# Tables for the order of each engine's instructions in the two attention layers of a trunk kernel

## The chip, the cores and the metric

One core of a Trainium2 chip runs the whole program. The metric is the device time of one execution in microseconds (us), the median over several executions. The engines are TensorE (PE: matmuls; PEld: its weight loads, which run beside the matmuls), VectorE (DVE), ScalarE (ACT), GpSimd (POOL) and SyncE (SP, which here only issues DMAs). Each engine takes its instructions strictly in the order in which they stand in its own stream and waits at the head of the stream until the operands of the next one are ready.

## What is computed

The input is x of 512 tokens by 1024 features. Two layers follow, an even one and an odd one, and each is a mixer and a feed-forward network (FFN) with an RMS norm ahead of both:

```python
for layer in range(DEPTH):                      # DEPTH = 2
    h = rms_norm(x, norm_mix_g[layer])
    x = x + (even_mixer if layer % 2 == 0 else odd_mixer)(h, ...)
    h = rms_norm(x, norm_ffn_g[layer])
    x = x + swiglu(h, ffn_w1[layer], ffn_w3[layer], ffn_w2[layer])
```

The even mixer has an attention of 8 heads in which each query sees only its 128 best keys, chosen by an index score (`relu(qi . ki)` summed over 4 index heads with weights `wi`), and a pooling of the projection `u` over windows of 2, 4, 8 and 16 tokens. The odd mixer has a stick-breaking attention of 16 heads: with `z = q . k`, the weight of a key is `exp(log_sigmoid(z) - sum of softplus(z) over the later keys)`. All products have fp32 inputs.

## The kernel before, in words

**Data.** x lies transposed in eight chunks `xs[0..7]` of 128 features by 512 tokens. Each fp32 operand of a large product is split into a high and a low part, and a product is three matmuls (high by high L205, high by low L206, low by high L207; in the FFNs L526 to L528 with 256 columns). Weights come by DMA on SP into three `raw` buffers, and are split by L177 to L181 and L188 in the mixers and L410/L411 in the FFNs.

**The norm.** `Norm.squared` adds the squares of the chunks on POOL (L280). `stats` multiplies the sum by ones on PE (L286), `ms` on DVE (L288) adds epsilon, and POOL takes the power of -1/2 into `rcol` (L291). `bcast` spreads `rcol` over the partitions with four matmuls (L297), and DVE copies that into `rb` (L307). Products run on the unscaled x, and `rb` is applied to what they give. For the FFN's norm, POOL and DVE also take sums and differences of the chunk pairs (L352 to L355), which the FFN's products read (L358).

**The even mixer** is a list of steps (`EVEN_ORDER`, L52), walked at L979. After the index projections `qi` and `ki` come `st` (stats) and `sb` (bcast), then `kj` (the index keys, scaled by `rb`), and `z(b)`: the scores of the query block b, of which there are four of 128. `sel(b, part)` finds the best 128 keys in 16 rounds of a maximum of eight (L770) and a replacement (L771) on DVE. `q(c, i)`, `nat` and `kn` make the queries, values and keys, `u(g, i)` and `y(g)` the pooling. `s(b, j, c)` is the score product of a block and head (L874 to L876), its maximum (L879, DVE), its exponential (L882, ACT) and its scaling; `pt` transposes it, `av` (L225, the helper `Bank.mm`) multiplies it with the values. `op(n)` adds the pooling's part of the output projection to chunk n, `oa(n)` the attention's part, and `oa(n)` then calls `chunk(n)` of the FFN's norm, from which its sums and squares start.

**The odd mixer** is a second list (`ODD_ORDER`, L74), walked at L1205. For each of eight chunks c of two heads there are `q(c, i)` and `k(c, i)` (24 matmuls each for both halves), `z(c, part)` for three parts A, B and C of the lower triangle, `e` (the softplus on ACT, DVE and POOL, split into `sh` and `sl`, L1139), `s` (the sum over later keys, matmuls that read `sh` and `sl`), `f` and `a` (the exponential, split into `ah` and `al`, L1167) and `o` (the product with the values). `x(h, n)` is the output projection.

**What sets the order.** The lists give the order in which the program is traced. The instructions of each engine are then laid out by the scheduler of the framework, which simulates the engines and takes, of the instructions that are ready, the one traced first. `follow` (L209) pins one instruction behind another on its engine without a semaphore. The FFN uses it once: `bcast` takes `after` (L293, called at L630), so that the four matmuls of `bcast` stand behind the products that `m` names.

Of the kernel before, what the change touches and what calls it, by code (L numbers as in the profile page):

```python
# [104 lines left out]
]  # L105
NEG = -1e30
GONE = -3e38
GONE_TEST = -2.5e38
# [8 lines left out]
def tile_trunk(ctx, tc, x, gains, qk_gain, pool_scale, w_a, w_nat, pool_w, w_o0, w_qk, w_v, w_o1, w13, w2, out):  # L117
    nc = tc.nc
    te, ve, ac, gp = nc.tensor, nc.vector, nc.scalar, nc.gpsimd
# [16 lines left out]
    def take(banks=range(8), n=1):  # L136

        free = [b for b in banks if all(i in given for i in range(b, b + n))]
        b = min(free, key=lambda b: max(given[i] for i in range(b, b + n)))
        ps = psum[:, b, :] if n == 1 else psum[:, b : b + n, :]  # L140
        for i in range(b, b + n):
            del given[i]
        taken[id(ps)] = ps, range(b, b + n)
        return ps

    def give(ps):
        for b in taken.pop(id(ps))[1]:
            given[b] = next(clock)
# [60 lines left out]
    def follow(m, first, why):  # L209

        tc.add_manual_dep(
            m.ins,
            first.ins.name,
            mybir.DependencyInfo(mybir.DependencyClass.NoSync, mybir.DependencyReason.DATA),
            reason=why,
        )
# [24 lines left out]
    class Norm:  # L241
# [48 lines left out]
            self.rcol = stat.tile([P, NB], F32, name=f"rcol{i}", tag="rcol")  # L290
            gp.tensor_tensor(self.rcol, ms, mhalf[:, 0:NB], op=ALU.pow)  # L291

        def bcast(self, banks=range(8), after=None):  # L293
            i = self.idx
            pb = take(banks)
            for b in range(NB):
                m = te.matmul(  # L297
                    pb[:, b * P : (b + 1) * P],
                    self.rcol[:, b : b + 1].to_broadcast([P, P]),
                    ident,  # L300
                    start=True,
                    stop=True,
                )
                if after is not None:
                    follow(m, after, "behind products that wait for less")
            self.rb = stat.tile([P, T], F32, name=f"rb{i}", tag="rb")
            ve.tensor_copy(self.rb, pb)  # L307
            give(pb)
# [53 lines left out]
    class Ffn:  # L362
# [13 lines left out]
        def open(self):  # L376
            self.nraw, self.nsplit = 0, 0
            self.fr = self.pool("fr", 1)
            self.fw = self.pool("fw", 2)
            self.fs = self.pool("fs", 1)  # L380
            self.steps = ffn(self)
# [20 lines left out]
    def ffn(stage):  # L402
        layer, nrm, nxt = stage.layer, stage.nrm, stage.nxt
# [219 lines left out]
        for f in range(1, NP):  # L623
            for w in range(2):
                x = Job(f, w)
                for who, p in ((x, 1), (x, 2), (y, 4), (x, 6), (y, 3), (x, 5), (x, 7)):
                    if who is not None:
                        m = who.prod(p)
                    elif p == 4:
                        nrm.bcast(after=m)  # L630
                        for d in start:
                            d.done()
                y = x
                q, r = divmod(f, 2)
                if q:
                    Down(q - 1, 2 * r + w)
# [13 lines left out]
    def even(nrm, nxt, w_first, after):  # L650
        with ExitStack() as es_wk:
# [23 lines left out]
            for j in range(2):  # L675
# [3 lines left out]
            gp.affine_select(  # L679
                bias[0], bias[0], pattern=[[-1, P]], base=0, channel_multiplier=1, compare_op=ALU.is_ge, fill=NEG  # L680
            )
# [84 lines left out]
            def step_sel(b, part):  # L766
# [5 lines left out]
                if part == NSEL // 32 - 1:  # L772
                    ve.tensor_scalar(bias[b], sc, GONE_TEST, NEG, op0=ALU.is_gt, op1=ALU.mult)

# [469 lines left out]
    ffns[1].run()  # L1244


# [1 line left out]
def _station(w):  # L1248

    k, m = w.shape  # L1250
    return w.reshape(k // 128, 128, m // 128, 128).transpose(2, 1, 0, 3).reshape(m // 128, 128, k)
# [51 lines left out]
```

## Time and profile before

| | |
|---|---|
| median of 3 runs | 1184.28 us (1182.9 to 1185.0) |
| the profiled execution's own time | 1183.68 us |
| span of its trace | 1181.9 us |
| granted TensorE clock, mean | 0.993 of full |
| busy: PE, PEld, DVE, ACT, POOL | 1143.6, 1005.8, 862.1, 606.1, 547.9 us |

The profiled execution lies 0.6 us below the median, and 1.8 us of it lie around the span. The even mixer fills the first 235 us or so, its FFN the time to about 540 us, the odd mixer that to about 860 us, and the second FFN the rest. Matmuls are pipelined, so one of 512 columns is shown with some 390 ns though the next one starts about 230 ns after it; a stretch in which PE is busy throughout can still hold matmuls that start late.

### The profile page before, as it was taken

To read this page: it belongs to the slowest core of one execution; us is meant where nothing else is said; L and a number is where in the kernel's file an instruction comes from. 1 tells how busy PE (TensorE), PEld (TensorE's weight loads), DVE (VectorE), ACT (ScalarE), POOL (GpSimd) and SP (SyncE) were. 2 spreads that over 40 slices of the span, in tenths; PEclk is the share of its full clock that TensorE was granted. 3 is DMA by queue.
4 is the path that set the end of the run, shared out by engine and by line. 5 is a ranking of instruction groups with operands and counts; after the bars stand their busy time and mean duration, and the time that the engine had idled before them with its cause. 6 is when DMAs were issued, how large, how long until landed. Compare 5 with 4: busy or idle time off the path is not lost.

```text
span 1181.9 us, 17814 instructions
## 1 busy us (share of the span) xinstructions
PE 1143.6 (97%) x6854; PEld 1005.8 (85%) x6856; DVE 862.1 (73%) x1180; ACT 606.1 (51%) x929; POOL 547.9 (46%) x506
## 2 busy tenths in 40 slices
PE   7998989999999999999999999999799999999998
PEld 4885747799999999998888888888699999999997
DVE  7699936688778677757467778877678877676764
ACT  5354566454444444436257788866354444444441
POOL 4166646766444444403033345434876444454420
PEclk9999999899999999999999999999999999999999
DMA  5221112123333333323321111114122332333321
GB/s 202 74 87 59 54 36 95 48 90 108 108 107 93 102 105 94 108 73 97 106 94 45 52 36 54 54 54 127 34 90 87 111 109 96 100 108 108 108 90 71
DMA packets 37667, 102.60 MB, mean 87 GB/s; under 512 B 4560, under 2 KB 7120, under 8 KB 37584
## 3 DMA queue, kind: packets, MB, share of 16 engines
q1 hardware_dynamic: 37152, 101.47, 27.5%
q8 instruction: 53, 0.87, 0.3%
q14 instruction: 30, 0.25, 0.1%
q10 hardware_dynamic: 432, 0.02, 0.0%
HBM read 99.37 MB, written 2.10 MB: 86 GB/s over the span
## 4 chain that ended last, share of the span: by engine, by line
PE 73%; DVE 9%; POOL 8%; issue 5%; ACT 3%; DMA 1%; SPq 0%; POOLq 0%; DVEq 0%; ACTq 0%
PE psum L526 10%; PE psum L528 10%; PE psum L527 10%; PE psum L205 10%; PE psum L206 10%; PE psum L207 10%; PE psum L225 6%; DVE score L771 1%; DVE m L770 1%; PE psum L1027 1%; PE psum L1028 1%; PE psum L1029 1%; POOL acc L280 1%; POOL s L494 1%; POOL s L492 1%
## 5 line engine op out<-in xcount | busy, mean ns | idle before, releaser
L599 DVE TENSOR_TENSOR x<-x,psum 128x512 f32<-128x512 f32 x88 | 60.4, 686 | 119.6 <-PE psum L207 119.4
L492 POOL TENSOR_TENSOR s<-raw_w 128x512 f32<-128x512 f32 x40 | 60.2, 1505 | 178.8 <-DMA raw_w<-in_w_dram 154.1
L206 PE MATMUL psum<-gsl,wh_w 128*128 128x512 f32 x352 | 137.7, 391 | 0.0
L207 PE MATMUL psum<-gsh,wl_w 128*128 128x512 f32 x352 | 135.4, 390 | 0.0
L205 PE MATMUL psum<-gsh,wh_w 128*128 128x512 f32 x352 | 135.2, 391 | 0.0
L577 POOL TENSOR_TENSOR c<-c,rb 128x512 f32<-128x512 f32 x40 | 61.2, 1530 | 118.3 <-ACT c L576 118.3
L410 ACT CAST wh_w<-raw_w 128x1024 fp32r<-128x1024 f32 (+1 forms) x48 | 47.0, 980 | 114.5 <-PE psum L206 106.6
L526 PE MATMUL psum<-hh,wh_t 128*128 128x256 f32 x320 | 90.1, 282 | 0.5 <-DVE c L559 0.5
L526 PE MATMUL psum<-hh,wh_a 128*128 128x256 f32 x320 | 90.1, 282 | 0.5 <-ACT wh_a L410 0.5
L528 PE MATMUL psum<-hh,wl_s 128*128 128x256 f32 x320 | 90.3, 283 | 0.0
L526 PE MATMUL psum<-hh,wh_s 128*128 128x256 f32 x320 | 90.3, 283 | 0.0
L527 PE MATMUL psum<-hl,wh_t 128*128 128x256 f32 x320 | 90.3, 282 | 0.0
L527 PE MATMUL psum<-hl,wh_s 128*128 128x256 f32 x320 | 89.9, 281 | 0.0
L527 PE MATMUL psum<-hl,wh_a 128*128 128x256 f32 x320 | 89.8, 281 | 0.0
L528 PE MATMUL psum<-hh,wl_t 128*128 128x256 f32 x320 | 89.7, 280 | 0.0
L528 PE MATMUL psum<-hh,wl_a 128*128 128x256 f32 x320 | 89.6, 281 | 0.0
L410 ACT CAST wh_a<-raw_w 128x1024 fp32r<-128x1024 f32 x40 | 42.0, 1050 | 71.8 <-PE psum L206 57.4
L207 PEld LDWEIGHTS psum<-gsh,wl_w 128*128 128x128 f32 x352 | 66.2, 188 | 12.9
L206 PEld LDWEIGHTS psum<-gsl,wh_w 128*128 128x128 f32 x352 | 66.2, 188 | 12.1
L205 PEld LDWEIGHTS psum<-gsh,wh_w 128*128 128x128 f32 x352 | 65.8, 188 | 11.8
L411 DVE TENSOR_TENSOR wl_a<-raw_w,wh_a 128x1024 fp32r<-128x1024 f32 x40 | 65.8, 1646 | 12.9 <-ACT wh_a L410 12.9
L411 DVE TENSOR_TENSOR wl_w<-raw_w,wh_w 128x1024 fp32r<-128x1024 f32 (+1 forms) x48 | 64.6, 1346 | 3.6 <-ACT wh_w L410 3.5
(357 smaller groups left out, 3780.7 us busy)
## 6 DMA issues: line engine op xcount, KB each, us to landing
raw_w<-in_w_dram SPq DMA_DIRECT2D x88, 512.0 KB, 3.6
raw_w<-in_w_dram SPq DMA_DIRECT2D x80, 256.0 KB, 3.0
raw_v<-in_w_v_dram SPq DMA_DIRECT2D x8, 512.0 KB, 3.7
raw_q<-in_w_qk_dram SPq DMA_DIRECT2D x8, 512.0 KB, 3.6
raw_k<-in_w_qk_dram SPq DMA_DIRECT2D x8, 512.0 KB, 3.7
raw_o<-in_w_o_dram SPq DMA_DIRECT2D x8, 512.0 KB, 3.6
x<-in_x_dram SPq DMA_DIRECT2D x8, 256.0 KB, 4.7
raw_q<-in_w_a_dram SPq DMA_DIRECT2D x4, 512.0 KB, 4.8
```

What stands on the lines that cost most here:

```text
L205: te.matmul(ps, wh, ah, start=(first and i == 0), stop=False)
L206: te.matmul(ps, wh, al, start=False, stop=False)
L207: te.matmul(ps, wl, ah, start=False, stop=(last and i == n - 1))
L225: m = te.matmul(dst, lhsT, rhs, start=self.first is None, stop=stop, skip_group_check=True)
L410: ac.copy(h[:, :n], src)
L411: ve.tensor_sub(l[:, :n], src, f32(h[:, :n]))
L492: gp.tensor_add(z[0], a21, a22)
L526: te.matmul(ps, wh, ah, start=first, stop=False, skip_group_check=True)
L527: te.matmul(ps, wh, al, start=False, stop=False, skip_group_check=True)
L528: m = te.matmul(ps, wl, ah, start=False, stop=(k == KC // 2 - 1), skip_group_check=True)
L577: gp.tensor_mul(d, d, nrm.rb)
L599: ve.tensor_add(xs[n], xs[n], self.ps[i])
```

## The change

The change adds a dictionary `ENGINE_ORDER` with one table for each engine, and at the end of the program, after everything is traced, pins each instruction that a table names behind the one that the table names before it, in the manner of `follow`. The numbers count the instructions of that engine in the order of tracing. `after` and its loop go from `bcast`. No instruction is added or taken away, and no operand changes.

The tables hold 3199 of the 6784 matmuls that are traced on PE, 662 of 1132 instructions on DVE, 560 of 890 on ACT, 355 of 507 on POOL and 110 of 314 on SP. Nearly all of the FFN's instructions are left out: on PE the table skips 1167 to 3107 almost entirely, and all from 5152 on. The order of SP's table is the one that SP had before. The matmuls of `bcast` of both FFN norms (932 to 935 and 4596 to 4599) are in the table.

```diff
+ENGINE_ORDER = {
+    "PE": (
+        "0-21 24-25 22-23 48-49 26-36 50-53 37-39 54-59 72 40-47 60-61 73-75 62-71 76-79 188-199 208-212 86 "
+        "84 90 88 80 87 89 81-83 85 91 213-219 104-112 232 128-130 233 131-133 113-115 152 92-93 116-127 "
...
+        "706-709 705 710-711 702-704 736 748 712 724-725 760 772 761 713-714 737-747 762-771 749-759 726 "
+        "715-723 727-735 773-778 808 779 811 780-781 809 812-813 782-783 823 796-797 784-785 824-825 835 810 "
...
+        "870 930-931 897 874 872-873 877-879 898 902-903 880-883 905-907 904 875-876 972-973 932-935 948 "
...
+        "3820 3735 3750-3751 3821-3825 3788 3826 3796 3740 3827-3831 3797-3798 3741-3742 3799-3802 3743 "
+        "3789-3794 3803-3806 3812-3817 3807-3809 3795 3744-3747 3856-3857 3818 3810 3858-3863 3836-3837 3811 "
...
+        "4551-4553 4557-4559 4563 4561 4564 4533 4582 4562 4566 4583 4567-4568 4594 4534 4544-4547 4538-4540 "
+        "4565 4569-4570 4595 4571 4500-4501 4511 4612-4613 4512-4513 4523-4525 4529-4531 4535-4536 4614-4617 "
+        "4600-4604 4596-4599 4537 4541-4542 4648 4618-4622 4543 4605-4611 4636-4638 4696-4697 4623 4649-4652 "
...
+    "DVE": (
+        "1 0 16-18 15 19 3-4 2 14 5-13 22 25 38-39 20-21 40 26 23 41-42 24 27 30 28-29 31-36 56 37 47 57 48 "
+        "68-75 81-88 95 58 96-98 59 99-102 123-131 43 89 44-45 60-61 105 46 62 52 143-144 49-50 115 53 51 "
...
+    "Pool": (
...
+        "111 110 106 115 120 112-113 147 114 148 129 116-118 138 121 123 122 125 124 126-128 130 132 131 "
+        "133-134 136 135 137 155 139 156 142 144 143 145 157 150-151 153 146 167-170 149 161 152 159-160 162 "
+        "154 158 163-166 173-176 172 179-180 171 181-182 177 185 183-184 186 178 270-272 277 276 278 273 279 "
...
+        "367 363-366 368-370 373 371-372 374 376-378 375 379-380 382-383 381 384-385 387 386 389 388 391 407 "
+        "405-406 408 390 395 393 392 396 394 401 399 397-398 400 402-404 411-412 409 413-414 410 417-420 416 "
...
-        def bcast(self, banks=range(8), after=None):
+        def bcast(self, banks=range(8)):
...
-                m = te.matmul(
+                te.matmul(
...
-                if after is not None:
-                    follow(m, after, "behind products that wait for less")
...
-                        nrm.bcast(after=m)
+                        nrm.bcast()
...
+    traced = [m for m in nc.cur_bb.bb.instructions]
+    for engine, runs in ENGINE_ORDER.items():
+        own = [m for m in traced if m.engine == getattr(mybir.EngineType, engine)]
+        places = []
+        for run in runs.split():
+            first, _, last = run.partition("-")
+            places += range(int(first), int(last or first) + 1)
+        for a, b in zip(places, places[1:]):
+            tc.add_manual_dep(
+                own[b],
+                own[a].name,
+                mybir.DependencyInfo(mybir.DependencyClass.NoSync, mybir.DependencyReason.DATA),
+                reason="order of the engine",
+            )
```

What the numbers of the lines shown stand for:

| engine | numbers: step |
|---|---|
| PE | 0-23 qi(0), 24-47 qi(1), 48-71 ki, 72-75 st, 76-79 sb, 80-83 kj, 84-91 z(1), 188-199 q(0,0), 208-219 q(0,1) |
| PE | 693-704 op(7), 705 and 710-711 last av, 712-723 oa(0), 724-735 oa(1), 736-747 oa(2), 748-759 oa(3), 760-771 oa(4), 772-783 oa(5), 796-807 oa(7), 808-879 and 884-907 the FFN's first two whole products, 880-883 its stats, 908-931 the next products, 932-935 its bcast |
| PE | 3740-3747 s(3,C), 3788-3803 s(3,B), 3804-3819 s(3,A), 3820-3831 k(4,1), 3856-3867 q(5,0) |
| PE | 4544-4547 stats of the second FFN, 4596-4599 its bcast |
| DVE | 27 rb copy, 28-29 the norm's square (L718, L719), 30 kif (L725), 34-37 z(1), 41-42 split of q_0, 56-57 split of q_1, 47-48 q(0,1), 68-75 and 81-88 and 95-102 and 123-130 sel(1, 0 to 3), 43-46 z(2) |
| POOL | 142-145, 150-153, 159-162: L352 to L355 of the pairs that oa(1), oa(3), oa(5) end; 146, 149, 154, 158, 163-165: L280 of chunks 1 to 7; 166: rcol; 167-170: L492 to L495 of the FFN's first weight sums, 173-176 of the next |
| POOL | 402-403: L280 of the last two chunks of the second FFN's norm; 404: its rcol; 405-408 and 411-414: L492 to L495 |

## Rows read from the trace of the kernel before

**Rows 1.** The page: busy time of the engines, and the chain that ended last.
```profile
PE 1143.6 (97%) x6854; PEld 1005.8 (85%) x6856; DVE 862.1 (73%) x1180; ACT 606.1 (51%) x929; POOL 547.9 (46%) x506
PE 73%; DVE 9%; POOL 8%; issue 5%; ACT 3%; DMA 1%; SPq 0%; POOLq 0%; DVEq 0%; ACTq 0%
```

**Rows 2.** Busy time by stretch: stretch, length, busy us of each engine, clock, DMA.
```profile
20.00:60.00 40.00, 38.93 (x228) 33.35 (x227) 27.52 (x51) 13.59 (x41) 4.87 (x4) 1.00 0.33 99
60.00:140.00 80.00, 74.39 (x360) 58.07 (x359) 78.29 (x210) 40.67 (x94) 54.84 (x74) 1.00 0.21 65
140.00:180.00 40.00, 36.46 (x152) 20.89 (x152) 15.84 (x40) 24.21 (x55) 18.32 (x29) 1.00 0.12 40
180.00:240.00 60.00, 57.42 (x274) 48.08 (x275) 41.92 (x41) 33.90 (x46) 45.86 (x33) 0.94 0.22 70
240.00:560.00 320.00, 320.00 (x2180) 297.09 (x2179) 235.48 (x295) 148.26 (x218) 142.59 (x101) 1.00 0.32 99
...
640.00:800.00 160.00, 154.56 (x836) 135.17 (x835) 128.21 (x138) 122.67 (x159) 70.08 (x85) 0.99 0.15 47
800.00:820.00 20.00, 20.00 (x90) 16.55 (x89) 14.80 (x18) 13.66 (x20) 5.36 (x5) 1.00 0.42 132
820.00:900.00 80.00, 72.85 (x452) 65.14 (x451) 61.08 (x65) 38.89 (x56) 59.60 (x41) 0.96 0.23 71
```

**Rows 3.** Timeline of DVE, 33 to 43 us: start, us, instruction, idle before.
```profile
34.69 0.16 DVE L718 TENSOR_TENSOR r<-rcol 128x4 f32<-128x4 f32 x1 [1.14 <-POOL rcol L291]
...
38.53 0.69 DVE L179 CAST wh_q<-raw_q 128x1024 fp32r<-128x1024 f32 x1 [3.47 <-PE psum L206]
```

**Rows 4.** Timeline of PE, 38 to 40 us.
```profile
38.33 0.39 PE L207 MATMUL psum<-hh,wl_q 128*128 128x512 f32 x1
38.55 1.05 PE L297 MATMUL psum<-ident,rcol 128*128 128x128 f32 x8
```

**Rows 5.** Timeline of DVE, behind the last sel, 149 us.
```profile
149.20 1.09 DVE L879 TENSOR_REDUCE mx<-psum 128x1 f32<-128x384 f32 x2 [2.90 <-PE psum L876]
```

**Rows 6.** POOL by line, 187 to 221.6 us: busy us, mean ns of one.
```profile
L280 POOL TENSOR_TENSOR acc<-acc,sq 128x512 f32<-128x512 f32 x7 | 12.4, 1777 | 0.1
```

**Rows 7.** Timeline of POOL, 187 to 229 us.
```profile
187.00 0.74 POOL L352 TENSOR_TENSOR b<-b 128x256 f32<-128x256 f32 x1 [12.92 <-PE psum L206]
...
193.13 1.30 POOL L280 TENSOR_TENSOR acc<-acc,sq 128x512 f32<-128x512 f32 x1
...
212.66 2.30 POOL L280 TENSOR_TENSOR acc<-acc,sq 128x512 f32<-128x512 f32 x1
...
225.36 2.26 POOL L492 TENSOR_TENSOR s<-raw_w 128x512 f32<-128x512 f32 x1 [3.83 <-DVE ms L288]
227.59 1.03 POOL L291 TENSOR_TENSOR rcol<-ms,mhalf 128x4 f32<-128x4 f32 x1
```

**Rows 8.** Timeline of PE, 221 to 235 us.
```profile
221.59 1.43 PE L286 MATMUL psum<-ones,acc 128*128 128x1 f32 x8 [1.99 <-POOL acc L280]
...
223.88 0.63 PE L207 MATMUL psum<-hh,wl 128*128 128x512 f32 x1
224.30 0.63 PE L205 MATMUL psum<-hh,wh 128*128 128x512 f32 x1
...
234.14 1.05 PE L297 MATMUL psum<-ident,rcol 128*128 128x128 f32 x8
```

**Rows 9.** What PE waited for, 640 to 800 us: total us, times, longest.
```profile
PE psum L225 <- DVE slB L1139: 3.8, 5, 1.1
```

**Rows 10.** Timeline of POOL, 845 to 857 us.
```profile
851.44 2.20 POOL L492 TENSOR_TENSOR s<-raw_w 128x512 f32<-128x512 f32 x1 [4.97 <-DVE wl_s L411]
...
855.80 1.01 POOL L291 TENSOR_TENSOR rcol<-ms,mhalf 128x4 f32<-128x4 f32 x1
```

**Rows 11.** What PE waited for, 800 to 900 us.
```profile
PE psum L297 <- POOL rcol L291: 2.4, 1, 2.4
```

**Rows 12.** Timeline of DVE, 705 us: a split of the odd layer.
```profile
705.43 1.80 DVE L1167 TENSOR_TENSOR alA<-aA,ahA 128x1024 fp32r<-128x1024 f32 x1
```

More of the change, by code (lines that the diff above doesn't have):

```diff
@@ L105 @@
 ]
+ENGINE_ORDER = {
[91 rows of a table added]
+    ),
+    "DVE": (
[24 rows of a table added]
+    ),
+    "Activation": (
[21 rows of a table added]
+    ),
+    "Pool": (
[12 rows of a table added]
+    ),
+    "SP": (
+        "9-18 23-25 33-34 26-32 35-36 39-42 37 55 38 56-58 60-61 59 65 62 66-68 70 69 71-72 74 73 75-78 "
+        "168-190 200-204 206 205 211 207-208 212-214 216 215 217-218 220 219 221-224 227-228 225-226 229-230 "
+        "232 231 233-236"
+    ),
+}
 NEG = -1e30
```

130 rows, old and new, of the table ENGINE_ORDER are left out of this document.

## The prediction

> **What bounds the kernel now.** Start with busy time: PE is busy 97% of the span, and 73% of the chain that ended last is PE [rows 1]. That is an average, so the second view is the same by stretch [rows 2]. In the FFNs PE is busy without a gap (320.00 of 320 us from 240 to 560); the tables leave those stretches alone, and an order can give nothing there. What is left is in the mixers and at their ends. PE idles 1.1 us of 20 to 60, 5.6 of 60 to 140, 3.5 of 140 to 180, 2.6 of 180 to 240, 5.4 of 640 to 800 and 7.2 of 820 to 900: 25.4 us together [rows 2]. But from 60 to 140 another engine sets the pace: DVE is busy 78.29 of 80 us [rows 2] with the top-k rounds. Idle PE is worth nothing there; what counts is how early DVE gets its first score, and how much else stands in front of the last round. DVE idles 12.5 us of 20 to 60 [rows 2], and that is where the even layer can gain. The third view, the timelines, names the waits.
>
> **How the change acts.** It adds no instruction, and its pins are without semaphores, so the price of the pins themselves is nothing. A matmul of 512 columns starts 0.22 us after the one before where nothing waits [rows 4]; I use 0.23 us for it and 0.117 us for one of 256 columns. SP's table repeats SP's old order, so no DMA is moved past another. Loads can only come later where a split that frees a raw buffer is moved back (that of q_1, places 56 and 57 of DVE, behind most of z(1)); the DMA engines are busy 0.33 of that stretch [rows 2], and PE has other products queued, so I cost it at nothing; without that cover one product would start some 2 us later. Removing `after` is covered too: the four matmuls of each bcast are places of the PE table.
>
> **Term 1, the head of the even layer: -4.6 us (2.0 to 6.0).** Before, rcol is there at 34.69 us, when DVE takes it, but the matmuls of bcast start at 38.55 [rows 3, 4]: they stand behind q(0,0) and q(0,1), 24 matmuls or 5.5 us. Meanwhile DVE waits 3.47 us for PE [rows 3]. In the table bcast (76-79) stands directly behind ki and ahead of q(0,0), stats (72) in the middle of ki, and z(1) behind five matmuls of q(0,1). On DVE the split of q_1 and the norm's square move behind what leads to z(1). So z(1), and sel(1,0) behind it, come some 5.5 us earlier: the 5.5 us of products leave the path. From there DVE is saturated, so an idle time taken away there arrives at the end of sel(3,3), less the work newly put in front: counted over DVE's stream with the durations of the trace, 128.5 us stand ahead of that end, against 127.7. That leaves 4.6. The lower end assumes that only half the 3.47 us and none of the rest goes; the upper one adds the 1.14 us wait for rcol. What is late next is DVE itself.
>
> **Term 2, the tail of the even layer: -2.5 us (0 to -3.5).** Behind the last top-k round DVE waits 2.90 us for a score product of block 2 [rows 5], because PE runs a filler product, op(7), first: 12 matmuls, 2.7 us. The table reduces those scores before sel(3,3) ends, and puts op(5) to op(7) later as filler between the transposes (702-704, the last of op(7), behind the last av). The idle of PE in the stretch, 3.5 us [rows 2], is the upper end; that the chain of exponentials bounds it anyway is the lower. I take the 2.7 us of op(7), less a little. After it PE is nearly the bound. [...]
>
> **Term 3, the first boundary: -1.0 us (+4.0 to -4.8).** From the last av at 179.9 us to bcast at 234.14 [rows 8] PE has 192 matmuls of 512 columns and 24 of 256, that is 47 us, so 6.6 us are lost: the wait of 1.99 us for the sum of squares [rows 8], and the half clock behind it. There matmuls start 0.42 us apart [rows 8], at a clock of 0.94 over the stretch [rows 2]; 14 of them cost 0.2 us each, 2.8 us. The new order starts with oa(2), oa(4), oa(3), oa(0), oa(1), so POOL's first pair is there after 63 matmuls (14.5 us) and not after 24 (5.5 us): at about 196 and not at 187.00 [rows 7]. The 24 operations that POOL then does without a pause took 34.6 us (187.00 to the stats at 221.59, [rows 7, 8]), and they are the same 24. So stats come at 230.5, and not at 221.6. Against that, rcol stands directly behind the last L280, ahead of L492 (2.26 us, [rows 7]), and PE reaches stats later too, because oa(7) and the next 24 products are placed before them. With the 3.83 us that POOL waited for ms shortened to 1 or 2, and 1.03 us for rcol [rows 7], bcast comes at 233 to 235. I take -1.0. The upper end of the gain is the wait and the half clock, 4.8 us; the lower one is POOL 4 us later with nothing to fill PE.
>
> **Term 4, the odd layer: -4.5 us (+3.0 to -7.2).** PE's waits here are for slB, 3.8 us in five waits [rows 9], and smaller ones of the same kind: 5.4 us in all by the idle of 640 to 800 [rows 2]. Each time the matmuls of s(c,B) that read sh are done before DVE has sl. The table cuts the products k(c+1, 1) into these places (for example 3820 to 3831 before and among 3788 to 3803: 12 matmuls, 2.8 us, against a wait of 1.1 us at most). I take five sixths of the idle. The upper end adds 1.8 us for the half clock that a shorter idle would spare; at the other end new waits cost 3 us more than the old.
>
> **Term 5, the second boundary: -3.2 us (0 to -4.8).** POOL does two weight sums, L492 and L494, from 851.44 until rcol starts at 855.80 [rows 10], and PE waits 2.4 us for that rcol [rows 11] and runs at half clock for some eight matmuls after it (0.8 us). The table puts rcol (404) directly behind the last L280 (403), and the sums behind it; PE still has 32 matmuls, 6 us, between stats and bcast. Both losses go: 3.2 us. Upper end: 1.6 us more of the waits ahead of stats; lower end: the next wait takes the place.
>
> **Sum.** 4.6 + 2.5 + 1.0 + 4.5 + 3.2 = 15.8 us off 1183.68, the profiled execution's own time, is 1167.9; the median of the runs stands 0.6 above it, so 1168.5. With all upper ends (26.3) it would be 1158.
>
> **Rivals.**
> 1. POOL's durations spoil both boundaries. One L280 took 1.30 us, another 2.30 [rows 7], with a mean of 1.78 [rows 6], though they do the same. The new order makes POOL's run the bound of the boundary, with no slack. If four more of the seven squares took 2.30 and the other sums 1.6 us more together, each boundary would lose 5.6 us: terms 3 and 5 become +4.6 and +2.4, the sum -4.6, the time 1179.7. Against it: the mix of work beside it hardly changes. [...] Chance 0.10.
> 2. The change does little: the old scheduler had put the instructions nearly so (on DVE, ACT and POOL a named instruction moves two or three places on average), and what is taken from one wait appears in the next. Then only part of term 1 is left: about 1183. Against it: on PE the mean move is 16 places, and the moves lie at the waits. Chance 0.08.
> 3. Slower: in the odd layer PE blocks at o(c, A). The table puts o(c, A) earlier and other products behind it. If a split comes late, PE can no longer take what was ready. The price of one round is the split on POOL and the one on DVE, 1.80 us [rows 12] and about 1 us, so 2.8 us; over eight rounds 22 us, in place of term 4. With the 11.3 us of the other terms it ends at 1195. It decides from 1.4 us a round. Against it: products of 2.8 us stand ahead of most of these places. Chance 0.12.
>
> **The numbers.** Forecast 0.70, at 1168.5, by itself from 1158 to 1178. The range takes in rival 1 and part of rival 2: 1157 to 1184. A measurement of this kernel can tell about 0.2% (2.4 us) from no change. Faster: 0.70 + 0.10 = 0.80; same: rival 2, 0.08; slower: 0.12.
>
> **What would show it.** Term 1: the matmuls of bcast start by 33.5 us, and the last round of sel(3,3) ends near 141.5. Term 2: no gap of 2.9 us on DVE behind it, and the last av at 172 to 174. Term 3: POOL's first L352 about 16 us behind the last av, bcast 53 to 54 behind it. Term 4: idle of PE in the odd layer near 1 us. Term 5: POOL goes from L280 to L291 with no sum between, and PE's wait for rcol below 1 us. The forecast is wrong if the FFN stretches change in length, if the sel rounds don't come earlier, or if PE waits at o(c, A).

## The result, and the profile after

The changed kernel takes 1199.15 us (median of 4, 1196.91 to 1199.5) against 1183.59 us (1181.93 to 1185.0) of the kernel before in the same comparison: a ratio of 1.0130, 95% interval 1.0113 to 1.0147. It is slower by 15.6 us, where 15 us less were forecast. The profiled execution has a span of 1197.8 us, 15.9 us more than before.

The page of the changed kernel, busy time:

```profile
PE 1151.3 (96%) x6856; PEld 999.9 (83%) x6856; DVE 870.7 (73%) x1180; ACT 607.4 (51%) x929; POOL 548.7 (46%) x506
```

The instructions are the same and so nearly is the busy time ([rows 1]); what has grown is the time in which PE does not get its matmuls started. Busy time by stretch of the changed kernel (columns as in [rows 2]):

```profile
43.40:150.50 107.10, 100.49 (x496) 76.86 (x495) 99.42 (x250) 51.90 (x132) 60.91 (x80) 0.98 0.20 61
150.50:178.80 28.30, 26.32 (x110) 14.56 (x109) 10.56 (x24) 17.72 (x40) 11.20 (x22) 1.00 0.07 19
178.80:234.20 55.40, 50.82 (x229) 40.16 (x228) 36.20 (x34) 29.04 (x41) 38.98 (x28) 1.00 0.28 86
234.20:300.00 65.80, 60.82 (x447) 56.52 (x446) 51.89 (x62) 32.61 (x50) 41.59 (x26) 1.00 0.29 89
300.00:556.00 256.00, 256.00 (x1736) 237.33 (x1735) 179.13 (x232) 113.18 (x165) 104.47 (x74) 1.00 0.33 101
556.00:640.00 84.00, 81.76 (x375) 66.62 (x374) 49.76 (x59) 39.22 (x57) 22.72 (x26) 0.98 0.28 82
640.00:800.00 160.00, 157.87 (x855) 135.38 (x854) 130.96 (x142) 130.37 (x168) 69.33 (x87) 1.00 0.17 50
...
868.00:945.00 77.00, 71.09 (x503) 65.45 (x503) 60.49 (x67) 35.64 (x53) 43.95 (x28) 1.00 0.27 83
```

The odd mixer (640 to 800) now has 2.1 us of idle PE, not 5.4. But the first 66 us of the first FFN have 5.0 us, those of the second 5.9, and the odd layer's start 2.2; before, PE's idle time in these three places was 0, 1.1 and 0 us.

Since idle time hides matmuls that start late, the runs below are compared by **lost time**: the length of a stretch, less 0.2272 us for each matmul of 512 columns that starts in it, 0.1172 for 256, 0.175 for 384 and 0.111 for fewer, which is close to the median spacing of such matmuls in the trace of before (0.227, 0.118, 0.178 and 0.109 to 0.112). The stretches end at the same instructions in every run, so their sums differ as the spans do (92.7 - 76.8 = 15.9 us). "Head" ends at the first round of sel(1,0), "top-k" at the mask behind sel(3,3), "tail" at the last copy of av, the boundaries at bcast of the FFN norm, the FFN heads 66 and 75 us behind that, "odd head" 30 us behind the first slB.

```
lost PE time, us      before   after   difference
head                   17.0     14.5     -2.5
top-k                  13.1     17.7     +4.6
tail                   12.4      9.1     -3.3
boundary 1              6.9      7.5     +0.6
FFN0 head               0.9      7.8     +6.9
FFN0 rest               1.9      1.9      0.0
odd head               -0.1      6.0     +6.1
odd body               10.1      6.4     -3.7
x(1, n) to bcast        9.0     10.6     +1.6
FFN1 head               3.9      9.2     +5.3
FFN1 rest               1.8      2.0     +0.2
```

The gains that were aimed at are there: head, tail and body of the odd mixer give 9.5 us. Four places take 22.9 us: the top-k stretch, the start of each FFN, and the start of the odd mixer.

Part of the lost time is TensorE's granted clock. In the trace of before it is 0.50 from 222.1 to 228.9 us, 669.3 to 672.6, 843.4 to 846.7 and 857.0 to 860.3, in that of the changed kernel from 88.8 to 92.1 us, 566.7 to 570.0 and 860.2 to 863.5, and 1.00 in the stretches between them, up to 1181.2 and 1197.8 us; such a spell is called half clock here. The length of a stretch times what its mean clock lacks of 1 gives about 3.6 us of 180 to 240, 1.6 of 640 to 800 and 3.2 of 820 to 900 before [rows 2], and in the changed kernel about 2.1 us of the top-k stretch, 1.7 of 556 to 640 and 2.0 of 800 to 868. So the clock does not make the changed kernel slower (its mean is 0.996, that of before 0.993). But a spell can be there in one trace and not in another of the same order: from 171 to 818 us the run `ffn1_pe` below has the order of before on PE, DVE, ACT and POOL. The window from 660 to 680 us, before and then in ffn1_pe:

```profile
660.00:680.00 20.00, 18.48 (x93) 16.11 (x91) 15.84 (x18) 13.79 (x18) 7.47 (x10) 0.91 0.18 54
660.00:680.00 20.00, 18.48 (x102) 15.93 (x101) 15.89 (x18) 15.25 (x20) 8.41 (x12) 1.00 0.19 54
```

PE is busy for the same 18.48 us and starts nine matmuls more. Differences of 1 to 2 us between single traces are therefore weak evidence.

### The profile page after: what moved, and what is told of

It is laid out like the page before. It is cut to its first block, busy times and chain, and to the rows that moved or that the text cites. A ratio compares the mean times of both kernels' runs of the same rounds, so it can differ in the third digit from the quotient of the medians.

```text
span 1197.8 us, 17779 instructions
## 1 busy us (share of the span) xinstructions
PE 1151.3 (96%) x6856; PEld 999.9 (83%) x6856; DVE 870.7 (73%) x1180; ACT 607.4 (51%) x929; POOL 548.7 (46%) x506
## 4 chain that ended last, share of the span: by engine, by line
PE 63%; POOL 7%; DVE 5%; issue 2%; ACT 1%; DMA 1%; POOLq 0%; DVEq 0%; ACTq 0%; SPq 0%
PE psum L687 9%; PE psum L689 9%; PE psum L688 9%; PE psum L368 9%; PE psum L370 9%; PE psum L369 9%; PE psum L388 6%; POOL s L653 1%; DMA raw_w<-in_w_dram 1%; PE psum L1188 1%; PE psum L1189 1%; PE psum L1190 1%; POOL s L654 1%; POOL s L656 1%; POOL s L655 1%
## 5 line engine op out<-in xcount | busy, mean ns | idle before, releaser
L653 POOL TENSOR_TENSOR s<-raw_w 128x512 f32<-128x512 f32 x40 | 65.4, 1634 | 159.4 <-DMA raw_w<-in_w_dram 142.4
L687 PEld LDWEIGHTS psum<-hh,wh_a 128*128 128x128 f32 x320 | 59.9, 188 | 7.6 <-ACT wh_a L571 3.1
```

The costliest lines, as they stand in the source:

```text
L653: gp.tensor_add(z[0], a21, a22)
L687: te.matmul(ps, wh, ah, start=first, stop=False, skip_group_check=True)
```

## The experiments

In each, the tables of the changed kernel are cut down, in unchanged order; what a table doesn't name is placed by the scheduler as before, and the numbers count traced instructions as in the section on the change. SP's table is kept in the first four runs only; the order of the DMAs is that of before in every trace, so it explains nothing here. Where FFN places are cut, `after` of `bcast` is put back:

```diff
-        def bcast(self, banks=range(8)):
+        def bcast(self, banks=range(8), after=None):
...
+                if after is not None:
+                    follow(m, after, "behind products that wait for less")
...
-                        nrm.bcast()
+                        nrm.bcast(after=m)
```

**1. Which part.** Four runs with one part of the tables each: without the FFNs' places, with these alone, with those of the even mixer, with those of the odd one. PE's lines at the seams of `mix_only`, the others are cut in the same way:

```diff
-        "715-723 727-735 773-778 808 779 811 780-781 809 812-813 782-783 823 796-797 784-785 824-825 835 810 "
+        "715-723 727-735 773-783 796-797 784-785 798-801 786-795 802-807 3120 3126 3121 3127-3129 3122 3130 "
```

mix_only:

> The tables with all places of both feed-forward networks taken out; the pin of bcast of the kernel before put back. Theory A (the loss comes from the tables' feed-forward places, which cut the first products of each FFN into small pieces of several products at once): the lost time of PE at the two FFN heads (7.1 and about 6.5 us more than before) goes, and the time is 1182 to 1187. Theory B (the mixers' tables leave ACT, DVE and POOL behind, and the FFN heads only inherit that): it stays near 1195 to 1199. Theory C (the loss is spread over new small waits everywhere): 1188 to 1193.

ffn_only:

> Only the feed-forward places of the tables, without the pin of bcast, the mixers in the order of the kernel before. Theory A: slower than before by 10 to 15 us, 1194 to 1199. Theory B: 1182 to 1187, as before. Theory C: 1186 to 1191.

even_only:

> Only the even mixer's places, pin of bcast put back. By the lost time of PE in the trace of the changed kernel the even mixer up to bcast is worth -0.7 us net (head -2.6, top-k stretch +5.3, tail -3.9, boundary +0.5). Theory A: 1181 to 1185, with the top-k rounds starting at 43 us and ending near 150. Theory B: 1188 to 1193, with new waits in the first FFN's head. Theory C: 1185 to 1190.

odd_only:

> Only the odd mixer's places. By the lost time of PE the odd mixer's body is worth -3.2 us, its head +5.4 and its end with the output projection +1. Theory A: 1182 to 1187, with the head's loss still there. Theory B: 1187 to 1192, the second FFN's head 4 us or more late. Theory C: 1184 to 1188.

Measured: mix_only 1189.93 us (ratio 1.0054, 1.0039 to 1.0069), ffn_only 1191.90 (1.0066, 1.0049 to 1.0083), even_only 1187.92 (1.0040, 1.0025 to 1.0055), odd_only 1183.40 (1.0003, 0.9993 to 1.0012). So the FFN places cost 8.3 us and the mixers' 6.3; 14.6 of the 15.6. By its range A holds for odd_only alone, C for mix_only and even_only, B for none, and ffn_only lies between the ranges of C and A. C's picture of small waits everywhere is wrong all the same: lost time shows four spots and little elsewhere. B has one of them right, the first FFN's head behind the even mixer's tables.

```
lost PE time, us          before  after  even_only  odd_only  mix_only  ffn_only
head, top-k and tail       42.5   41.3     41.3       42.6      41.4      43.6
boundary 1 and FFN0 head    7.8   15.3     14.6        7.5      14.6       8.9
odd head                   -0.1    6.0     -0.1        2.4       2.4       0.3
odd body                   10.1    6.4      8.6        6.5       6.5      10.1
FFN1 head                   3.9    9.2      3.9        4.6       4.6       9.6
```

The loss at the first FFN's head comes with the **even mixer's** places (14.6 us without any FFN place); the one at the second FFN's head comes with the FFN places (9.6) and not with the odd mixer's (4.6). That ffn_only loses 1.1 us more in the even mixer, where it has no place, goes with a granted clock of 0.91 from 80 to 100 us (before 1.00). The split between boundary 1 and the FFN's head hangs on where bcast lies (1.3 and 7.6 us in ffn_only, 7.9 and 6.7 in even_only), so their sum is given. The first FFN's places were not run by themselves.

The odd mixer's gain in its body is its own, and its head takes 2.5 us of it back. The other 3.6 us of the head come when odd and FFN places stand together: the changed kernel then runs the last products of the FFN among those of v, which before all came ahead of v; PE waits once, 1.8 us, for the x that DVE adds up, and from 566.7 to 570.0 us the clock is 0.50. What PE waited for, 550 to 640 us, and the window from 560 to 575 us:

```profile
PE psum L1188 <- DVE x L760: 1.8, 1, 1.8
```

```profile
560.00:575.00 15.00, 13.19 (x53) 10.35 (x52) 9.91 (x11) 6.07 (x8) 5.69 (x8) 0.89 0.24 70
```

The wait and 15 us at 0.89 (about 1.6 us) make 3.4 us.

**2. The first boundary.** `even_cut` keeps the even table as far as the last av, without the steps oa; `oa_pe` adds PE's places of oa to that and none of the other engines'.

```diff
-        "706-709 705 710-711 702-704 736 748 712 724-725 760 772 761 713-714 737-747 762-771 749-759 726 "
+        "706-709 705 710-711 702-704"
```

> The even table as far as the last av, without the steps oa (whose order decides when the chunks of the FFN's norm are ready). Theory P (the new order of oa delays POOL's sums, so stats, rcol and rb come some 10 us later, and the first FFN's head pays): the lost time of PE from the last av to 66 us behind bcast falls back from 15.4 us (even mixer's table whole) to about 8.6 (before), and the time is 1180 to 1183. Rival Q (what the even table leaves undone on ACT and DVE is paid in the FFN's head whatever the order of oa): it stays above 12 us, 1185 to 1189.

> The even table as in even_cut (1181.6), and in addition PE's places of the steps oa, with ACT, DVE and POOL free there. Theory P1 (PE's order of oa, with chunk 1 fifth, is what delays POOL's sums): first L352 at about 193 us, stats at 229 to 232, lost time of PE over boundary and FFN head back at 12 us or more, 1185 to 1188. Theory P2 (it is the order on POOL, DVE and ACT): below 10 us, 1181 to 1183.

Measured: even_cut 1181.62 us (0.9979, 0.9970 to 0.9989), oa_pe 1187.24 (1.0031, 1.0021 to 1.0041). The lost time over boundary and FFN head is 7.3 us in even_cut and 13.1 in oa_pe. Timelines of POOL, first of even_cut, then of oa_pe: the first L352 (other line numbers, same instruction, `b<-b`).

```profile
186.94 0.74 POOL L399 TENSOR_TENSOR b<-b 128x256 f32<-128x256 f32 x1 [2.16 <-ACT b L392]
```

```profile
195.40 0.74 POOL L400 TENSOR_TENSOR b<-b 128x256 f32<-128x256 f32 x1 [1.17 <-ACT b L393]
```

So P and P1 hold: it is PE's order of the steps oa. That chunk 1's fifth place in it is the point, is read from these starts and was not varied by itself. The same place in the changed kernel, timeline of POOL:

```profile
193.80 0.74 POOL L513 TENSOR_TENSOR b<-b 128x256 f32<-128x256 f32 x1 [9.85 <-ACT b L506]
...
219.50 8.92 POOL L443 TENSOR_TENSOR acc<-acc,sq 128x512 f32<-128x512 f32 x5
232.92 1.02 POOL L454 TENSOR_TENSOR rcol<-ms,mhalf 128x4 f32<-128x4 f32 x1 [4.50 <-DVE ms L451]
235.52 2.21 POOL L653 TENSOR_TENSOR s<-raw_w 128x512 f32<-128x512 f32 x1 [1.58 <-DVE wl_s L572]
```

POOL starts 15.0 us behind the last av and not 7.1, and does its squares until 228.4. As rcol stands ahead of the weight sums, bcast still starts at 234.2, where it was (in oa_pe, where POOL is free to take a weight sum first, at 238.65). The price falls later: the next weight sum starts at 235.52 and not at 225.36 [rows 7], 10 us late, and PE, which has meanwhile used up the products that needed nothing, waits. What PE waited for, 234 to 300 us (before: nothing to 300):

```profile
PE psum L368 <- DVE x L760: 1.4, 1, 1.4
PE psum L687 <- DVE g L626: 1.2, 1, 1.2
PE psum L687 <- ACT u L697: 1.0, 1, 1.0
PE psum L687 <- ACT wh_s L571: 0.7, 1, 0.7
```

These are weight splits and the emptying of banks, the work of DVE and ACT. The chain that ended last, from 234 to 300 us, is PE alone before; in the changed kernel a third of it is POOL's weight sums (L653 to L656):

```profile
by line: DMA raw_w<-in_w_dram 13.3%; POOL s L653 12.6%; POOL s L654 9.4%; issue 9.1%; POOL s L655 6.7%; POOL s L656 4.5%; DVE wl_s L572 3.8%; DVE wl_b L663 3.7%; DVE gsl L598 3.4%; ACT wh_s L571 3.0%; DVE x L760 2.8%; POOL c L624 2.3%; DVE 
```

That the splits are late because POOL's sums and rb are late is argued from this, not shown: the chain of ffn_only looks alike, and there boundary and head together lose only 1.1 us more than before. That PE's order of oa brings the loss of the two stretches is shown.

**3. The even mixer itself.** `head_only` has the places as far as z(1), `no_head` is even_cut without them, `tail_only` has the last top-k rounds, the scores and av of blocks 2 and 3, and op(4) to op(7). PE's part of head_only is

```diff
-        "84 90 88 80 87 89 81-83 85 91 213-219 104-112 232 128-130 233 131-133 113-115 152 92-93 116-127 "
+        "84 90 88 80 87 89 81-83 85 91"
```

> Only the tables' places as far as z(1): bcast ahead of q(0,0), early z(1). Theory D (DVE is saturated from 52 to 146 us, so an idle time that is taken away ahead of it arrives at the end of sel(3,3)): sel(1,0) starts near 43 us, sel(3,3) ends at 140 to 142, time 1178 to 1181. Rival R (the work that was put off comes back in between, with gaps and collisions of DVE and POOL): sel(3,3) ends at 144 to 147, time 1182 to 1185.

> even_cut (1181.6) without its places as far as z(1). Theory S (the stretch's loss, 13.1 to 19.0 us of PE's time, comes with the early top-k rounds, which hold DVE while the softmax chain of 32 items waits for it): the stretch is back at 13 to 15 us, tail at 9.5, and the time is 1177 to 1181. Rival T (the middle of the even table costs it by itself): the stretch stays at 17 us or more, the head's 3 us are lost, 1183 to 1186.

> Only the places of the last two query blocks: the last top-k rounds, scores, transposes and av of blocks 2 and 3, and op(4) to op(7). If the tail's gain (12.4 to 9.5 us of lost PE time) is its own: 1180 to 1182. If it only moves work out of the stretch before: 1183 to 1186.

Measured: head_only 1186.38 us (1.0020, 1.0011 to 1.0029), no_head 1192.11 (1.0066, 1.0049 to 1.0083), tail_only 1186.02 (1.0022, 1.0009 to 1.0035).

head_only is the telling one. sel(1,0) starts at 43.8 us and the mask behind sel(3,3) is there at 139.5, 6.1 us earlier, as theory D had it; and yet the last av is at 182.7 and not at 179.9. The two times that matter are when the mask of block 3 is made (DVE) and when PE first uses it in a score. Timeline of DVE and then of PE, the kernel before:

```profile
145.61 0.43 DVE L773 TENSOR_SCALAR bias<-score 128x512 bf16<-128x512 f32 x1
...
155.92 0.39 PE L876 MATMUL psum<-bias,identb 128*128 128x512 bf16 x1
```

The same two of head_only:

```profile
139.52 0.43 DVE L789 TENSOR_SCALAR bias<-score 128x512 bf16<-128x512 f32 x1
...
160.47 0.39 PE L892 MATMUL psum<-bias,identb 128*128 128x512 bf16 x1
```

The mask lay ready for 9.9 us before, and for 20.5 us in head_only. **The end of the top-k rounds does not set the end of the even mixer.** Up to the last av PE starts 137 to 138 us of matmuls in each of these traces, by the spacings above; the rest is lost time, and the mixer ends earlier only by what PE loses less. Windows from the mask to the last av, before and then in head_only:

```profile
145.60:179.90 34.30, 30.85 (x128) 17.07 (x128) 10.57 (x28) 22.13 (x49) 13.55 (x24) 1.00 0.10 37
139.50:182.70 43.20, 39.84 (x173) 24.85 (x173) 12.64 (x31) 24.62 (x56) 24.74 (x33) 1.00 0.14 49
```

PE has 45 matmuls more to do behind the mask in head_only, for in the top-k stretch it lost 19.2 us and not 13.1. Most of these 6.1 us can be put down to the clock, which before was 1.00 from 80 to 140 us. Windows of head_only:

```profile
80.00:100.00 20.00, 17.00 (x81) 13.32 (x79) 19.75 (x51) 6.40 (x15) 16.61 (x22) 0.91 0.19 56
100.00:120.00 20.00, 16.74 (x63) 11.03 (x63) 18.72 (x54) 8.22 (x23) 7.16 (x18) 0.89 0.18 57
120.00:139.50 19.50, 19.50 (x83) 13.67 (x82) 18.75 (x46) 10.60 (x24) 7.43 (x13) 0.94 0.09 28
```

That is up to 5.2 us. It is no accident of one execution: the mean clock of the ten of head_only is 0.985 to 0.992, that of even_cut's ten 0.992 to 0.995. Why it falls there is open. D's time is missed by 5 us, and R, with its gaps and collisions, in both its numbers.

The rest of PE's lost time here is put down to the chain of 32 scores (block by block, through two banks: product, maximum on DVE, exponential on ACT, then the next), whose maxima run from 84.4 to 171.2 us before, from 77.6 to 173.9 in head_only, 87.4 to 170.7 in even_cut. That early top-k rounds take DVE from these maxima is argued, not shown.

no_head and tail_only speak on what was still open. S falls: without the head's places the top-k stretch still loses 17.2 us, so the early rounds are not its only source, and the head loses 24.4 us, at the seam of pinned and free instructions: one wait of 4.4 us, and a clock of 0.53 from 42 to 50.3 us. What PE waited for, 20 to 60 us:

```profile
PE psum L780 <- ACT wit L769: 4.4, 1, 4.4
```

T's expectation of the stretch holds; its time is missed by that seam. In tail_only, which ends at the edge of its second range, the stretch loses 19.1 us and the tail 9.7: the tail's gain is work moved from one to the other. Over head, top-k and tail together the lost time is 42.5 us before, 42.6 in even_cut, 41.3 in the changed kernel, 45.2 in head_only, 45.9 in tail_only. The even mixer's table gains a microsecond at most.

**4. The odd mixer.** `odd_body` has the odd mixer's places without its head and without x(1, n), `odd_no_v` all of them but v, stats, bcast and ve; `cut_odd` is even_cut with the odd mixer's places. The first line of PE's table in odd_body:

```diff
-        "3120 3126 3121 3127-3129 3122 3130 3123-3124 3131 3150 3125 3144 3132-3134 3151-3153 3145-3149 "
+        "3384-3387 3424 3432 3388-3392 3433 3425-3427 3434 3464-3471 3428-3431 3435-3439 3393-3407 3416 3408 "
```

> Only the odd mixer's places behind its head (no v, stats, bcast and nothing of chunk 0's q, k, z, e) and ahead of x(1, n). If the body's gain of 3.7 us (lost time of PE from 640 to 800 us, 18.4 to 14.8) is its own: 1179 to 1181. If it only comes with the head's order, which costs 2.5 us: 1182 to 1184.

> odd_only (1183.4) without the places of v, stats, bcast and ve. Theory U (the head's 2.5 us come from bcast and v being cut into each other): they go, the body keeps 6.5 us in place of 8.5 to 10, and the time is 1180 to 1182. Rival V (a partly pinned head fits no schedule, as in odd_body): 1184 or more.

> even_cut (1181.6) and the odd mixer's places (odd_only, 1183.4, -0.5) together. If the parts add: 1180 to 1182, the best so far. If they meet in the first FFN or in the DMA order: above 1184.

Measured: odd_body 1196.14 us (1.0107, 1.0085 to 1.0129), odd_no_v 1185.19 (1.0009, 0.9998 to 1.0020), cut_odd 1183.51 (0.9993, 0.9984 to 1.0002). The body loses 6.3 to 6.5 us of PE time in all three, so its gain is its own: 3.7 us against the trace of before, 2.1 against ffn1_pe, whose body has the order of before and a clock of 1.00 from 660 to 680 us. None of the three kernels could keep it. odd_body misses both its ranges by 12 us and more: pinned and free instructions meet at the seam, PE stood still once for 6.6 us, with a clock of 0.86 from 620 to 645 us (before 1.00), and the second FFN's head lost 8.7 us in place of 3.9. What PE waited for, 545 to 660 us:

```profile
PE psum L284 <- DVE eA L1193: 6.6, 1, 6.6
```

U falls: without v and bcast the head still loses 2.8 us. V holds, with its 1184 or more. cut_odd lies between its two ranges, 1.5 us above what was hoped of it; its lost time is 75.2 us, with even_cut's 74.9, so the odd mixer's places add nothing.

**5. The second FFN's head.** `ffn1_only` has that FFN's places alone, `ffn1_pe` PE's part of them, `ffn1_rest` the part of ACT, DVE and POOL.

```diff
-    "PE": (
-        "0-21 24-25 22-23 48-49 26-36 50-53 37-39 54-59 72 40-47 60-61 73-75 62-71 76-79 188-199 208-212 86 "
...
+    "PE": (
+        "4475-4477 4487-4489 4499 4478 4481 4479 4482 4472 4480 4490 4584 4473-4474 4484-4486 4496-4498 4483 "
...
```

> Only the places of the second FFN, no other table. If its pieces (single products cut into each other) cost the 5.8 us of its head by themselves: 1188 to 1190. If the loss needs the first FFN's or the odd mixer's places ahead of it: 1182 to 1185.

> Of the second FFN's places only PE's. Theory I (the cutting of products into single matmuls on PE costs the 5.5 us that ffn1_only lost in this head): lost time in the head 8 to 10 us as in ffn1_only, 1187 to 1190. Theory J (the order of ACT, DVE and POOL there costs it): 4 to 5.5 us as before, 1182 to 1185.

> Of the second FFN's places only those of ACT, DVE and POOL. Theory I: 1182 to 1185, lost time in the head near 4 us. Theory J: 1187 to 1190, near 9 us.

Measured: ffn1_only 1189.09 us (1.0035, 1.0019 to 1.0051), ffn1_pe 1197.82 (1.0114, 1.0099 to 1.0129), ffn1_rest 1192.40 (1.0079, 1.0056 to 1.0103). Lost time of this head: before 3.9, ffn1_only 9.4, ffn1_pe 18.7, ffn1_rest 13.5. So the places cost 5.5 us by themselves, and I and J both fall: each half alone is worse than the two together. What PE waited for, 855 to 960 us, in ffn1_only and then in ffn1_pe:

```profile
PE psum L567 <- ACT wh_s L451: 2.2, 1, 2.2
PE psum L569 <- DVE wl_b L543: 1.5, 1, 1.5
```

```profile
PE psum L552 <- DVE x L625: 4.1, 1, 4.1
PE psum L552 <- ACT u L562: 1.7, 2, 1.1
```

In the order of before the 12 matmuls of a product mostly stood together. In the table products are cut into each other in pieces of one to twelve matmuls, most of them of one to three, the weights of several jobs are wanted at once, and PE waits for a split (wh_s, wl_b). Whether the cutting or the order of the splits is the first cause, these runs don't settle.

**A faster version.** even_cut, at 0.9979 of the kernel before, is the best of all 15 and beats both; its 2.3 us are hardly more than a measurement can tell. Its interval lies clear of 1, but its table is not shown to be the reason. Of its lost time 0.5 us less fall at the first boundary, and 1.6 us less in the odd mixer, where it has no place: that part is put down to the spell of half clock that the trace of before has at 669.3 to 672.6 us (0.91 from 660 to 680 us, in ffn1_pe 1.00).

## Why the prediction was wrong

The forecast was 1168.5 us, in a range from 1157 to 1184; measured were 1199.15.

**"An idle time taken away there arrives at the end of sel(3,3)"** (term 1) held in head_only and not in the changed kernel. bcast and rb did come 8 us earlier (rb at 32.86 and not 41.30), sel(1,0) 9 us. The changed kernel, timeline of DVE:

```profile
32.86 0.69 DVE L468 COPY rb<-psum 128x512 f32<-128x512 f32 x1
...
43.44 0.43 DVE L931 MAX8 m<-score 128x8 f32<-128x256 f32 x1
```

In head_only, where only this is changed, sel(3,3) ended 6.1 us earlier. In the changed kernel it ended 4.4 us later, which the prediction had named as a sign of being wrong. It had counted 5.5 us less idle time on DVE ahead of that end and 0.8 us more work. The windows up to the mask, before and then after (DVE is the third number with a count), show 18.7 and 18.5 us of idle time, and 4.6 us more busy time:

```profile
0.00:145.60 145.60, 130.31 (x632) 101.36 (x633) 126.94 (x292) 68.96 (x156) 79.08 (x121) 1.00 0.30 95
0.00:150.05 150.05, 135.35 (x648) 103.93 (x649) 131.57 (x295) 71.78 (x164) 76.24 (x121) 0.99 0.28 90
```

What was taken from the head came back between the rounds.

The step that failed is the one behind it: that the end of sel(3,3) sets the end of the mixer, and so that "idle PE is worth nothing there". The trace of before held the answer, a mask that lay for 9.9 us. "DVE is busy 78.29 of 80 us" made DVE the bound, and whose work ahead of the last av ended last was left open. The even mixer ended 1.2 us early with rounds that ended late, by what PE lost less (41.3 us for 42.5). -4.6 for term 1 was worth at most 1, and **term 2** (-2.5) the same microsecond: its 3.3 us in the tail had been lost in the stretch before.

**Term 3** had the size of POOL's delay nearly right and the sum wrong. The first L352 came 15.0 us behind the last av (forecast 16), bcast 55.4 us (forecast 53 to 54, before 54.2). That bcast stands at 234.2, as forecast, is luck: 233 to 235 was counted from a last av at 179.9, and it came at 178.8. The half clock went as forecast (0.50 from 222.1 to 228.9 us before, now 1.00 from 178.8 to 234.2), but other waits took its place, 7.5 us lost for 6.9 (the prediction's 6.6 would be 7.2 by its own figures). And the account ended at bcast, as if PE's queue beyond were free: with POOL 10 us late, the FFN's head lost 6.9 us more. The term should have been about +7.

**Term 4** was right in mechanism; its size, -4.5, came out at -3.7 in the body, of which 1.6 is the spell of half clock that not every trace of the order of before has (0.91 from 660 to 680 us before, 1.00 in ffn1_pe). That a shorter idle spares half clock, as its upper end had it, was an estimate and is not shown: in the trace of before PE stood idle for 2.31 us up to 100.50, and the clock was 1.00 from 98.2 to 104 us. PE's waits for slB and shB fell from 4.6 to 1.5 us. The changed kernel, what PE waited for, 640 to 800 us:

```profile
PE psum L388 <- POOL shB L344: 1.2, 2, 0.8
PE psum L388 <- DVE slB L1300: 0.3, 1, 0.3
```

The head of the odd mixer, 6.1 us, had no term. **Term 5**: rcol went first, and PE's wait for it is gone, but of 3.2 us nothing was left. From x(1, n) to bcast 1.6 us more were lost (PE waited 4.5 us for hl and 1.5 for the sum of squares, before 3.6 and 0), and then 5.3 in the FFN's head.

**"The tables leave those stretches alone"** was the costliest sentence. The tables hold 1039 FFN matmuls, nearly all of them in the heads of the two FFNs. PE lost 0.9 and 3.9 us there before, so a new order had little to give and much to take; the prediction priced it at nothing, because PE was busy there without a gap. By themselves these places cost 8.3 us, and it was one of its signs of being wrong that the FFN stretches change in length.

**The rivals.** Rival 3 had the sign and a time of 1195, for a reason that did not come: PE's waits in the odd body are 1.9 us in all, none for o(c, A). Rival 1 had the place (the boundary) but not the cause: POOL's seven squares took 12.5 us, as before; it was the start that was late. That the change does not do what it says is unlikely: from rb at 32.86 to MAX8 at 43.44 us DVE's instructions stand in the order of its table (27 30 28-29 31-36 56 37 47 57 48 68).

The removal of `after` was not tried without the tables; in the changed kernel bcast stands where its places put it. The second FFN's head loses as much with `after` in place (ffn1_only, 9.4 us) as without it (9.2).

## What to carry to other kernels

An engine that is busy all through a stretch need not set the end of it: look for a result that lies ready, and follow back what its user was waiting for. Add up the work of the engine that ends the stretch; the time that it loses is all that a new order can give. Look at the granted clock before two traces are compared by a microsecond or two. Follow a moved step beyond the first wait that it satisfies, to the engine that does it and to what that engine owes next; the boundary's price was paid in the 66 us behind it. And an order that leaves the bound engine hardly a gap has little to give: in the second FFN's head, pinned whole or by half of the engines, it lost 5.5 to 14.8 us of PE time here.

## What was not expected of the hardware

A small operation on DVE lasted here until a large one on POOL beside it had ended. In the kernel before, adding a constant to 128x8 elements (L860) took 147 to 526 ns; in the changed one it took 306 to 1352. The timeline of DVE in the changed kernel, and then that of POOL:

```profile
80.56 1.35 DVE L1021 TENSOR_SCALAR rq<-rq 128x8 f32<-128x8 f32 x1
86.87 1.11 DVE L1021 TENSOR_SCALAR rq<-rq 128x8 f32<-128x8 f32 x1
92.30 1.02 DVE L1021 TENSOR_SCALAR rq<-rq 128x8 f32<-128x8 f32 x1
```

```profile
79.15 2.73 POOL L351 TENSOR_TENSOR wl_u<-raw_u,wh_u 128x1024 fp32r<-128x1024 f32 x1
...
85.61 2.35 POOL L351 TENSOR_TENSOR wl_u<-raw_u,wh_u 128x1024 fp32r<-128x1024 f32 x1 [1.98 <-ACT wh_u L340]
...
91.14 2.15 POOL L1095 TENSOR_TENSOR s<-s 128x512 f32<-128x512 f32 x2
```

Each of the three ends within 0.04 us of the POOL operation under it, the third of the second of two (81.91 and 81.88, 87.98 and 87.96, 93.32 and 93.29): as these rows read, DVE's operation was held until POOL's was done; by what, they don't show. From the first round of sel(1,0) to the mask the same DVE operations took 3.0 us longer in the changed kernel by net, and the four of L860 alone 2.8.
